# Feed-forward weight sums one column pair ahead, S4 in the buffer of S2, and the evacuation of ad behind the next block's first copy

## The chip, the cores and the metric

The kernel runs as one program on one core of a Trainium2 chip. The core has five engines with a queue each: PE (TensorE), DVE (VectorE), ACT (ScalarE), POOL (GpSimd) and SP (SyncE, which here only issues DMAs). The metric is device time in microseconds (us) of one execution. Before the change it is 3349.23 us, the median of three runs between 3341.76 and 3353.75.

## The reference, cut to what matters

The reference is one inference step of a one-layer encoder: a mixing sub-layer (attention and gated linear attention) and then a gated feed-forward sub-layer. The change lies in the feed-forward alone, on T = 2048 + 32 tokens, D_MODEL = 1024 and D_FF = 2816:

```python
def conv_ffn(h, conv_state, w_up, w_dw, b_dw, w_down):
    t = h.shape[1]
    u = h @ w_up
    uu = jnp.concatenate([conv_state.astype(u.dtype), u], axis=1)
    y = b_dw
    for j in range(CONV_W):
        y = y + w_dw[j] * uu[:, j:j + t]
    a, g = jnp.split(y, 2, axis=-1)
    out = (jax.nn.gelu(a, approximate=True) * g) @ w_down
    return out, uu[:, -(CONV_W - 1):]
```

All is float32. Each float32 operand of a product is split into a high and a low part, and a product is three passes (high times high, high times low, low times high).

## The kernel before, in words

**Units and blocks.** The tokens are cut into six segments, and two segments are worked on at a time (p = 0, 1, 2). Both feed-forward matrices are multiplied by a Strassen-like scheme: the weight matrix is seen as 2x2 quarters A11, A12, A21, A22, the activations as quarters B, and a pair of output columns over a pair of segments takes seven products instead of eight. The seven weight operands are A11, A12, A22 and four sums: S1 = A21 + A22, S2 = S1 - A11, S3 = A11 - A21, S4 = A12 - S2. A *block* is one pair of output columns m of one unit u. Units 0 to 2 are the up-projection for p = 0, 1, 2 with 22 blocks each; units 3 to 11 are the down-projection, for each p in three groups of rows, with 4 blocks each. That is 102 blocks; each has seven products of 12 matmuls (9 where a group has three row tiles).

**The weights of a column.** The generator `weights()` (L1476) serves the operands. The first time a column is met (p = 0: unit 0 and units 3 to 5, 34 columns, called *fresh* below) SP loads the four quarters from HBM (L1490) into four of eight raw buffers (`raws`, 256 KB each), POOL makes S1, S2 and S3 (L1512, three instructions, S3 in the place of A21), and DVE makes S4 in the place of A12 (L1512). Every operand is then split: the high part by ACT (L67), the low part by DVE (L70), into slots named ring, hA and hB. The four sums are stored to HBM (sW, sD; L1515) and loaded again for p = 1 and p = 2, where neither POOL nor the S4 subtraction has work. POOL's three sums of a column stand at the start of the column's own turn in this generator, and they write buffers that S4 (once A12) and A22 of the column before have just left.

**A block** (L1644 to L1699) runs on two accumulators in PSUM, `ad` and `g`. Product A11 goes to ad; ACT copies it to g (L1656); then follows A22, the last product of the block before, into that block's g, with its convolution and gating on ACT and DVE (`up_g`, L1607); then S2 to g, a copy of g to U2 (L1662), S1 to ad, a copy P5 (L1665), S3 to g, an add on DVE (L1668), A12 to ad, S4 to ad, an add on DVE (L1679). After it the block's ad is evacuated: in the up-projection a convolution of width 3 (ACT L1575, then twice DVE L1577) and a gelu on ACT (L1687); in the down-projection a sum into an accumulator (`down_sum`, L1620). Every second block `act_sums` (L1599 to L1602) makes sums of two columns of activations on DVE in place, which must wait until the store of those activations has landed. Seven times in a block `side()` lets the work beside the blocks take one step: stores that were put off (L1590), the rest of the mixing sub-layer at the start, one step of `weights()` (one split), one step of the activation operands, and the work after a unit.

**What sets the order.** PE's order is written out by hand (a manual schedule for that engine alone). For ACT, DVE, POOL and SP a scheduler sets the order from the program. Within an engine instructions run in that order, one after the other.

Of the kernel before, what the change touches and what calls it, by code (L numbers as in the profile page):

```python
# [26 lines left out]
MF = 22  # L27
# [31 lines left out]
def encoder_step(ctx: ExitStack, tc: tile.TileContext, I, O):  # L59
# [520 lines left out]
    with ExitStack() as st:  # L580
# [188 lines left out]
        def step(gen):  # L769
            if gen is not None:  # L770
                next(gen, None)
# [690 lines left out]
    def raw(i, n=4):  # L1462
        return raws_[:, 512 * i:512 * i + 128 * n].rearrange("p (k n) -> p k n", n=128)
# [12 lines left out]
    def weights():  # L1476


        todo = []
        for u, (p, g) in enumerate(UNITS):  # L1480
            for m in range(NM[u]):
                todo += [(u, m, x) for x in (("A21", "A22", "A11", "A12") if p == 0 else WOPS)]
        at = {}

        def fetch():

            while todo and free and len(at) < NRAW - 2:
                u, m, x = todo.pop(0)
                at[u, m, x] = i = free.pop(0)
                nc.sync.dma_start(raw(i, NK[u]), w_rows(u, m, x))  # L1490

        freed = []

        def refill():

            free.extend(freed)
            freed.clear()
            fetch()

        def part(u, m, x, i):  # L1500
# [9 lines left out]
        def total(u, m, eng, op, out, a, b):  # L1510
            n = NK[u]
            getattr(eng, op)(raw(out, n), raw(a, n), raw(b, n))  # L1512

        def keep(u, m, x, i):
            nc.sync.dma_start(w_rows(u, m, x), raw(i, NK[u]))  # L1515

        fetch()
        for u, (p, g) in enumerate(UNITS):
            for m in range(NM[u]):
                if p == 0:  # L1520
                    a11, a12, a21, a22 = [at.pop((u, m, x)) for x in ("A11", "A12", "A21", "A22")]
                    free.extend(freed)
                    freed.clear()
                    s1, s2 = free.pop(0), free.pop(0)
                    total(u, m, nc.gpsimd, "tensor_add", s1, a21, a22)
                    total(u, m, nc.gpsimd, "tensor_sub", s2, s1, a11)
                    total(u, m, nc.gpsimd, "tensor_sub", a21, a11, a21)
                    fetch()
                    for x, i in zip(WOPS, (a11, s2, s1, a21, a12, a12, a22)):
                        if x == "S4":  # L1530
                            total(u, m, nc.vector, "tensor_sub", a12, a12, s2)
                            freed.append(s2)
                        yield from part(u, m, x, i)
                        if x == "S1":
                            keep(u, m, "S2", s2)
                        if x in SUM and x != "S2":
                            keep(u, m, x, i)
                        yield
                        refill()
                        if x not in ("S2", "A12"):  # L1540
                            freed.append(i)
                else:
                    for x in WOPS:
                        i = at.pop((u, m, x))
                        yield from part(u, m, x, i)
                        yield
                        refill()
                        freed.append(i)

    wq = weights()  # L1550

# [55 lines left out]
    def up_g(p, m, g, ya, before):  # L1607

        o = WP[p] - 2
        conv(YG, g, m + MF, o)  # L1610
        nc.vector.tensor_mul(ya[:, :, :o], ya[:, :, :o], YG[:, :, :o])
        defer(1, actD[p, m, :, :, :o], ya[:, :, :o])
        if m % 2:
            made.append((p, m // 2, before, ya))
# [29 lines left out]
    def block(u, m, prev, side):  # L1644
# [24 lines left out]
        last = u == len(UNITS) - 1 and m == NM[u] - 1  # L1669
        if last:  # L1670
            down_sum(p, grp, m + 4, g, False, 1)
        if u == 2:
            conv_outputs(g[:, 1], m + MF)
# [6 lines left out]
        if u == 2:  # L1680
            conv_outputs(ad[:, 1], m)
        if grp is None:
            YA.append(YA.pop(0))
            before, ya = YA[-2:]
            o = w - 2
            conv(ya, ad, m, o)
            nc.scalar.activation(ya[:, :, :o], ya[:, :, :o], AF.Gelu_apprx_tanh)  # L1687
        else:
# [96 lines left out]
    def hstep():  # L1785
        while hq and next(hq[0], 1) == 1:
            hq.pop(0)
# [137 lines left out]
```

## Time and profile before

| | us |
|---|---|
| median of three runs | 3349.23 |
| profiled execution, device time | 3328.72 |
| its span, first to last instruction | 3327.0 |
| mean granted TensorE clock in it | 0.981 |
| PE busy, share of the span | 3134.7, 94% |
| DVE busy | 2264.7, 68% |
| ACT busy | 1673.4, 50% |
| POOL busy | 573.0, 17% |

All times in the rows below are from this one execution. The feed-forward takes from about 1813 us to the end. Unit 0 with its 22 blocks lies between about 1840 and 2209 us, unit 1 between 2209 and 2514, unit 2 between 2514 and 2819, units 3 to 5 begin at 2819. PE's clock is full (1.00) in most of it, and the busy share of PE is high, so what can be had lies in the stretches where PE waits.

### The profile page before, as it was taken

How to read it: one execution, taken by the hardware profiler on the slowest of the kernel's cores; microseconds unless marked ns; L12 is line 12 of the kernel's file. 1: busy time of each engine (PE TensorE's matmuls, PEld its weight loads, DVE VectorE, ACT ScalarE, POOL GpSimd, SP SyncE). 2: the span in 40 equal slices, each digit the busy share in tenths (PEclk: the TensorE clock that was granted, in tenths of full speed). 3: DMA queues.
4: the chain of work that ended last, by engine and by line, in shares of the span. 5: the costliest groups of instructions: out<-in, count | busy, mean ns of one | idle time of the engine just before them, and what ended most of it. 6: DMA issues, size and time to landing. Idle time of an engine off the chain costs nothing. (4 is left out here: it accounts for less than half of the span.)

```text
span 3327.0 us, 58007 instructions
## 1 busy us (share of the span) xinstructions
PE 3134.7 (94%) x19928; PEld 2979.6 (90%) x19928; DVE 2264.7 (68%) x4858; ACT 1673.4 (50%) x3835; POOL 573.0 (17%) x687
## 2 busy tenths in 40 slices
PE   6999999999999999899999798999999999899996
PEld 5899998888999999889988787999999999899996
DVE  6725527664545555754777887887778778788886
ACT  4412224443455545533545644465556656566755
POOL 3102101111111111112444323210000001221011
PEclk8999999999999999999999999999999999999998
DMA  7334434445333333654565786576668666769794
GB/s 216 113 121 142 128 110 120 126 129 138 107 109 113 111 106 114 206 169 155 166 213 172 234 263 223 189 238 193 185 183 242 192 191 194 232 208 294 222 284 125
DMA packets 601370, 580.25 MB, mean 174 GB/s; under 512 B 55761, under 2 KB 529570, under 8 KB 601074
## 3 DMA queue, kind: packets, MB, share of 16 engines
q1 hardware_dynamic: 556386, 528.93, 53.1%
q10 hardware_dynamic: 44432, 47.34, 4.4%
q8 instruction: 157, 2.57, 0.3%
q14 instruction: 139, 1.14, 0.1%
q0 software_dynamic: 256, 0.26, 0.0%
HBM read 388.71 MB, written 187.65 MB: 173 GB/s over the span
## 5 line engine op out<-in xcount | busy, mean ns | idle before, releaser
L76 PE MATMUL pm<-hA,wh 128*128 128x416 f32 x768 | 288.2, 375 | 0.0
L67 ACT ACTIVATE hA<-raws 128x512 fp32r<-128x512 f32 (+1 forms) x320 | 196.5, 617 | 180.7 <-PE ad L1561 96.8
L77 PE MATMUL pm<-hA,wh 128*128 128x416 f32 x768 | 269.4, 351 | 0.0
L78 PE MATMUL pm<-hA,wl 128*128 128x416 f32 x768 | 269.2, 351 | 0.0
L1561 PE MATMUL ad<-hA,hB 128*128 128x350 f32 (+2 forms) x1533 | 264.4, 323 | 0.9 <-ACT work L1665 0.7
L1561 PEld LDWEIGHTS ad<-hA,hB 128*128 128x128 f32 x1533 | 249.4, 189 | 1.8 <-ACT work L1665 1.7
L1512 POOL TENSOR_TENSOR raws<-raws 128x512 f32<-128x512 f32 (+1 forms) x102 | 147.6, 1460 | 587.2 <-DVE g L1571 284.6
L70 DVE TENSOR_TENSOR hA<-raws,hA 128x512 fp32r<-128x512 f32 (+1 forms) x320 | 229.6, 720 | 28.0 <-ACT hA L67 26.8
L67 ACT ACTIVATE hB<-raws 128x512 fp32r<-128x512 f32 (+1 forms) x240 | 147.0, 616 | 131.2 <-PE ad L1561 68.0
L934 POOL TENSOR_SCALAR P<-P,mx 128x640 f32<-128x640 f32 (+5 forms) x136 | 101.3, 745 | 544.0 <-DVE mx L933 269.1
L1561 PE MATMUL g<-hA,hB 128*128 128x350 f32 (+2 forms) x954 | 171.8, 330 | 20.4 <-ACT g L1656 9.7
L1561 PE MATMUL ad<-hA 128*128 128x350 f32 (+2 forms) x1047 | 182.9, 325 | 2.0 <-ACT work L1665 2.0
L70 DVE TENSOR_TENSOR hB<-raws,hB 128x512 fp32r<-128x512 f32 (+1 forms) x240 | 168.6, 705 | 22.9 <-ACT hB L67 20.8
L1561 PEld LDWEIGHTS g<-hA,hB 128*128 128x128 f32 x954 | 157.6, 192 | 26.5 <-ACT g L1656 13.4
L76 PE MATMUL pn<-wh,hA 128*128 128x256 f32 (+1 forms) x624 | 177.8, 285 | 0.0
L1561 PE MATMUL ad<-hA,hA 128*128 128x348 f32 (+2 forms) x1014 | 177.8, 325 | 0.0
L78 PE MATMUL pn<-wh,hA 128*128 128x256 f32 (+1 forms) x624 | 176.7, 283 | 0.0
L77 PE MATMUL pn<-wl,hA 128*128 128x256 f32 (+1 forms) x624 | 176.7, 283 | 0.0
L1561 PEld LDWEIGHTS ad<-hA 128*128 128x128 f32 x1047 | 171.8, 191 | 2.3 <-ACT work L1665 2.3
L1561 PE MATMUL ad<-hA,ring 128*128 128x348 f32 (+2 forms) x978 | 169.5, 324 | 1.3 <-ACT work L1665 1.3
L67 ACT ACTIVATE pth<-pp 128x256 fp32r<-128x256 f32 (+1 forms) x288 | 106.1, 373 | 126.3 <-PE pp L1001 116.3
L1561 PEld LDWEIGHTS ad<-hA,hA 128*128 128x128 f32 x1014 | 166.6, 191 | 0.1
(437 smaller groups left out, 9168.9 us busy)
## 6 DMA issues: line engine op xcount, KB each, us to landing
raws<-in_w_up_dram SPq DMA_DIRECT2D x220, 256.0 KB, 3.7
raws<-sW SPq DMA_DIRECT2D x176, 256.0 KB, 3.0
sW<-raws SPq DMA_DIRECT2D x88, 256.0 KB, 3.2
raws<-in_w_down_dram SPq DMA_DIRECT2D x80, 256.0 KB, 4.6
wr<-in_w_in_dram SPq DMA_DIRECT2D x76, 256.0 KB, 3.4
sgT<-tx ACTq DMA_DIRECT2D x80, 208.0 KB, 2.3
wa<-in_w_ada_dram SPq DMA_DIRECT2D x64, 256.0 KB, 3.1
keys<-ks SPq DMA_DIRECT2D x128, 128.0 KB, 2.9
```

Source lines behind the costliest of these rows:

```text
L67: i = nc.scalar.activation(hi, src, AF.Copy)
L70: nc.vector.tensor_sub(lo, src, f32(hi))
L76: nc.tensor.matmul(out, ah, bh, start=first and i == 0, stop=False)
L77: nc.tensor.matmul(out, ah, bl, start=False, stop=False)
L78: nc.tensor.matmul(out, al, bh, start=False, stop=last and i == n - 1)
L934: nc.gpsimd.tensor_scalar(P[:m, :tot], P[:m, :tot], mx[:m, 6:7], 1.0, op0=OP.mult, op1=OP.mult)
L1512: getattr(eng, op)(raw(out, n), raw(a, n), raw(b, n))
L1561: nc.tensor.matmul(out[:, :w], l_[:, k], r_[:, k, :w], start=first and k == 0 and i == 0, stop=k == n - 1 and i == 2, skip_group_check=True)
```

## The change

It has five parts. (1) `weights()` is written anew: POOL's sums of the next fresh column (`total3`) are issued before the S4 split of the current one, and not at the start of their own column; S1 and S2 take the buffers that S3 and A12 of the current column leave. (2) S4 is written into the buffer of S2 and not of A12, right before the split of S3, and every sum is stored as its own split is issued. (3) Loads may run at most to the next column, but may use all eight buffers. (4) In `block()` the convolution (or `down_sum`) of ad moves into `rest()`, which the next block calls after its first copy; the outputs of the convolution's state move with it. (5) In `side()` the step of the activation operands comes before that of the weights.

```diff
+        def total3(c):
+            free.extend(freed)
+            freed.clear()
+            at[c, "S1"], at[c, "S2"] = s1, s2 = free.pop(0), free.pop(0)
+            at[c, "S3"] = a21 = at.pop((c, "A21"))
+            total(c, nc.gpsimd, "tensor_add", s1, a21, at[c, "A22"])
+            total(c, nc.gpsimd, "tensor_sub", s2, s1, at[c, "A11"])
+            total(c, nc.gpsimd, "tensor_sub", a21, at[c, "A11"], a21)
...
-            while todo and free and len(at) < NRAW - 2:
+            while todo and free and todo[0][0] <= cur + 1:
...
-        for u, (p, g) in enumerate(UNITS):
-            for m in range(NM[u]):
-                if p == 0:
-                    a11, a12, a21, a22 = [at.pop((u, m, x)) for x in ("A11", "A12", "A21", "A22")]
-                    free.extend(freed)
-                    freed.clear()
-                    s1, s2 = free.pop(0), free.pop(0)
-                    total(u, m, nc.gpsimd, "tensor_add", s1, a21, a22)
-                    total(u, m, nc.gpsimd, "tensor_sub", s2, s1, a11)
-                    total(u, m, nc.gpsimd, "tensor_sub", a21, a11, a21)
-                    fetch()
-                    for x, i in zip(WOPS, (a11, s2, s1, a21, a12, a12, a22)):
-                        if x == "S4":
-                            total(u, m, nc.vector, "tensor_sub", a12, a12, s2)
-                            freed.append(s2)
-                        yield from part(u, m, x, i)
-                        if x == "S1":
-                            keep(u, m, "S2", s2)
-                        if x in SUM and x != "S2":
-                            keep(u, m, x, i)
...
+        for cur in range(len(cols)):
+            u, m = cols[cur]
+            for x in WOPS:
+                if x == "A11" and fresh[cur] and (cur, "S1") not in at:
+                    total3(cur)
+                if x == "S3" and fresh[cur]:
+
+                    at[cur, "S4"] = at[cur, "S2"]
+                    total(cur, nc.vector, "tensor_sub", at[cur, "S4"], at[cur, "A12"], at[cur, "S4"])
+                if x == "S4" and cur + 1 < len(cols) and fresh[cur + 1]:
+                    total3(cur + 1)
+                i = at[cur, x]
+                yield from part(cur, x, i)
+                if fresh[cur] and x in SUM:
+                    nc.sync.dma_start(w_rows(u, m, x), raw(i, NK[u]))
+                yield
+                refill()
+                if not (fresh[cur] and x == "S2"):
+                    freed.append(i)
...
     def up_g(p, m, g, ya, before):
 
         o = WP[p] - 2
+        if p == 2:
+            conv_outputs(g[:, 1], m + MF)
         conv(YG, g, m + MF, o)
...
-        if u == 2:
-            conv_outputs(ad[:, 1], m)
-        if grp is None:
-            YA.append(YA.pop(0))
-            before, ya = YA[-2:]
-            o = w - 2
-            conv(ya, ad, m, o)
-            nc.scalar.activation(ya[:, :, :o], ya[:, :, :o], AF.Gelu_apprx_tanh)
-        else:
+        if last:
             down_sum(p, grp, m, ad, m == 0)
         side()
 
         def rest():
+            if grp is None:
+                YA.append(YA.pop(0))
+                before, ya = YA[-2:]
+                o = w - 2
+                if u == 2:
+                    conv_outputs(ad[:, 1], m)
+                conv(ya, ad, m, o)
+                nc.scalar.activation(ya[:, :, :o], ya[:, :, :o], AF.Gelu_apprx_tanh)
+            elif not last:
+                down_sum(p, grp, m, ad, m == 0)
             prod(g[:, 0], u, m, "A22", "T4", False)
...
         issue()
         step()
+        hstep()
         next(wq, None)
-        hstep()
         pend()
```

Every engine executes the same number of instructions as before, and PE's order is the same matmul for matmul. What moves on the other engines is shown at three places in the middle of unit 0. (The line numbers shift: POOL's and DVE's sums are at L1512 before and at L1499 after; the copy of ad to g is L1656 and L1654; the convolution on ACT L1575 and L1571, on DVE L1577 and L1573; gelu L1687 and L1688.)

First POOL, with the semaphores each row waits for, the three sums of one column of unit 0. Before:

```order
L1512 TENSOR_TENSOR raws<-raws 128x512 [waits DMAHW6_49,DMAHW7_49,DMAHW2_49,DVE_49]
L1512 TENSOR_TENSOR raws<-raws 128x512 [waits DMAHW2_49,DVE_49,Pool_49]
L1512 TENSOR_TENSOR raws<-raws 128x512
```

And after, the three of the same column:

```order
L1499 TENSOR_TENSOR raws<-raws 128x512 [waits DMAHW1_49,DMAHW0_49,DMAHW4_49,DVE_49,Pool_49]
L1499 TENSOR_TENSOR raws<-raws 128x512 [waits DMAHW3_49,Pool_49]
L1499 TENSOR_TENSOR raws<-raws 128x512 [waits DVE_49]
```

Before, the first row waits for the low part of the previous column's S4 on DVE and for the landing of that S4's store, since it writes S4's buffer. After, the first row waits for the previous column's S3 (its split and its store), and one sum, now S2 in the third row, for the low part of the previous column's A12 on DVE; both splits stand ahead of that of S4, which is the sixth of the column's seven.

Second DVE, in the middle of unit 0 around column 15: `hB_677`, `hA_104` and `ring` are slots of the split operands, L70 is the low part of a split. Before:

```order
L70 TENSOR_TENSOR hB_677<-raws,hB_677 128x512 [waits PE_49,Activation_49]
L1577 SCALAR_TENSOR_TENSOR work<-ad,cw,work 128x2x348 [waits DVE_49]
L70 TENSOR_TENSOR hA_104<-raws,hA_104 128x512 [waits PE_49,Activation_49]
L1577 SCALAR_TENSOR_TENSOR work<-g,cw,work 128x2x348 [waits Activation_49]
L70 TENSOR_TENSOR hA_104<-raws,hA_104 128x512 [waits PE_49,Activation_49]
L1577 SCALAR_TENSOR_TENSOR work<-g,cw,work 128x2x348 [waits DVE_49]
L70 TENSOR_TENSOR ring<-raws,ring 128x512 [waits DMAHW4_49,PE_49,Activation_49]
L1611 TENSOR_TENSOR work<-work 128x2x348 [waits DVE_49]
L1668 TENSOR_TENSOR g<-g,work 128x350 [waits PE_49,Activation_49]
L1600 TENSOR_TENSOR work<-work 128x348 [waits DVE_49]
L1512 TENSOR_TENSOR raws<-raws 128x512
```

And after:

```order
L70 TENSOR_TENSOR hB_677<-raws,hB_677 128x512 [waits PE_49,Activation_49]
L1573 SCALAR_TENSOR_TENSOR work<-ad,cw,work 128x2x348 [waits DVE_49]
L70 TENSOR_TENSOR hA_104<-raws,hA_104 128x512 [waits PE_49,Activation_49]
L1499 TENSOR_TENSOR raws<-raws 128x512 [waits DMAHW4_49,DMAHW0_49,DVE_49]
L1573 SCALAR_TENSOR_TENSOR work<-g,cw,work 128x2x348 [waits Activation_49]
L70 TENSOR_TENSOR hA_104<-raws,hA_104 128x512 [waits PE_49,Activation_49]
L1573 SCALAR_TENSOR_TENSOR work<-g,cw,work 128x2x348 [waits DVE_49]
L70 TENSOR_TENSOR ring<-raws,ring 128x512 [waits PE_49,Activation_49]
L1609 TENSOR_TENSOR work<-work 128x2x348 [waits DVE_49]
L1666 TENSOR_TENSOR g<-g,work 128x350 [waits PE_49,Activation_49]
L1596 TENSOR_TENSOR work<-work 128x348 [waits DVE_49]
```

The sum S4 (L1512, now L1499) moves seven instructions forward, to right behind the low part of S2, and where it had no wait it now waits for two DMAs: the load of A12 and the store of S2.

Third ACT, around the first copy of the same block. Before:

```order
L1575 ACTIVATE work<-ad,cw 128x2x348
L67 ACTIVATE hB_677<-raws 128x512
L1656 COPY g<-ad 128x350
L67 ACTIVATE hA_104<-raws 128x512
L1687 ACTIVATE work<-work 128x2x348
L1575 ACTIVATE work<-g,cw 128x2x348
L67 ACTIVATE hA_104<-raws 128x512
L1662 COPY work<-g 128x350
```

And after:

```order
L1571 ACTIVATE work<-ad,cw 128x2x348
L67 ACTIVATE hB_677<-raws 128x512
L1654 COPY g<-ad 128x350
L67 ACTIVATE hA_104<-raws 128x512
L1688 ACTIVATE work<-work 128x2x348
L1571 ACTIVATE work<-g,cw 128x2x348
L67 ACTIVATE hA_104<-raws 128x512
L1660 COPY work<-g 128x350
```

Here nothing moved: the convolution of ad stands ahead of the first copy as it did. The same holds in the middle of units 0 and 1; in about half the blocks of unit 2 it now stands behind the copy.

On SP the loads and stores are the same ones, with the four loads of a column next to each other and the stores of one S4 and of the next column's S1 to S3 in a row.

## Rows read from the trace of the kernel before

**Rows 1.** The stretches of the feed-forward: start and end in us, length, busy us of PE, PEld, DVE, ACT and POOL with instruction counts, then the granted TensorE clock as a share of full speed, the DMA share and GB/s.

```profile
1840.00:1920.00 80.00, 61.45 (x332) 58.44 (x332) 72.36 (x114) 52.63 (x96) 31.35 (x29) 0.89 0.73 227
1920.00:2057.00 137.00, 119.52 (x684) 116.42 (x682) 114.15 (x165) 65.74 (x110) 37.27 (x34) 0.94 0.79 249
2057.00:2209.00 152.00, 140.00 (x840) 134.80 (x840) 124.48 (x176) 80.95 (x138) 39.38 (x26) 1.00 0.63 199
2209.00:2514.00 305.00, 297.61 (x1842) 294.29 (x1843) 241.96 (x367) 178.26 (x300) 0.27 (x4) 1.00 0.69 199
...
2819.00:2990.00 171.00, 155.24 (x918) 152.30 (x919) 134.75 (x185) 100.99 (x183) 45.93 (x33) 0.96 0.69 215
```

**Rows 2.** The same view for the copy L1656 alone, which is executed once a block: the count in brackets is the number of blocks.

```profile
1840.00:1920.00 80.00, 1.78 (x4) 0.89 0.73 227
1920.00:2057.00 137.00, 3.58 (x8) 0.94 0.79 249
2057.00:2209.00 152.00, 4.46 (x10) 1.00 0.63 199
2209.00:2514.00 305.00, 9.87 (x22) 1.00 0.69 199
...
2819.00:2990.00 171.00, 5.32 (x13) 0.96 0.69 215
```

**Rows 3.** What PE waited for, by stretch (total us, times, longest us): two rows of 1840 to 1920, two of 1920 to 2057, two of 2057 to 2209, one of 2209 to 2514, and two of 2819 to 2990.

```profile
PE g L1561 <- ACT work L1662: 11.7, 4, 5.6
PE g L1561 <- ACT g L1656: 3.7, 3, 1.7
...
PE g L1561 <- ACT g L1656: 7.8, 4, 3.0
PE g L1561 <- ACT work L1662: 5.0, 2, 2.6
...
PE g L1561 <- ACT g L1656: 8.0, 7, 1.7
PE g L1561 <- ACT work L1662: 3.1, 5, 1.5
...
PE g L1561 <- ACT g L1656: 7.3, 8, 1.4
...
PE g L1561 <- ACT work L1662: 11.0, 5, 3.2
PE g L1561 <- ACT g L1656: 5.5, 4, 3.4
```

**Rows 4.** The timeline from 2098.6 to 2106.5 us, a block in the middle of unit 0: start, length, engine, line, operation, and in brackets the idle time before it with what ended it. L1512 on DVE is the sum S4, on POOL S1 to S3 of the next column.

```profile
2098.74 0.68 DVE L1512 TENSOR_TENSOR raws<-raws 128x512 f32<-128x512 f32 x1
...
2099.45 0.34 SPq L1515 DMA_DIRECT2D sW<-raws  x1
...
2103.55 4.34 POOL L1512 TENSOR_TENSOR raws<-raws 128x512 f32<-128x512 f32 x3 [10.74 <-DVE hA L70]
2104.87 0.63 ACT L67 ACTIVATE hB<-raws 128x512 fp32r<-128x512 f32 x1 [1.56 <-POOL raws L1512]
2105.41 0.44 ACT L1656 COPY g<-ad 128x350 f32<-128x350 f32 x1
...
2105.90 0.91 PE L1561 MATMUL g<-hA,hA 128*128 128x350 f32 x4 [0.92 <-ACT g L1656]
```

**Rows 5.** The timeline around 2088 us, the block before that one.

```profile
2087.53 0.52 DVE L1599 TENSOR_TENSOR work<-work 128x348 f32<-128x348 f32 x1 [1.62 <-DMA actD<-work]
2087.97 0.52 DVE L1679 TENSOR_TENSOR ad<-ad,work 128x350 f32<-128x350 f32 x1
...
2088.53 0.93 ACT L1575 ACTIVATE work<-ad,cw 128x696 f32<-128x696 f32 x1 [2.26 <-DVE ad L1679]
...
2090.48 2.20 PE L1561 MATMUL g<-hA,hA 128*128 128x350 f32 x12 [0.90 <-ACT g L1656]
```

**Rows 6.** The timeline from 2837 us, a block of unit 3 (down-projection).

```profile
2838.69 0.63 ACT L67 ACTIVATE ring<-raws 128x512 fp32r<-128x512 f32 x1 [1.32 <-POOL raws L1512]
...
2841.19 0.46 ACT L1662 COPY work<-g 128x348 f32<-128x348 f32 x1
...
2841.70 1.53 PE L1561 MATMUL g<-hA,hA 128*128 128x348 f32 x4 [2.74 <-ACT work L1662]
```

**Rows 7.** What ACT waited for from 1840 to 2209 us (total us, times, longest us), its rows on POOL's sums and on the add L1679.

```profile
ACT work L1575 <- DVE ad L1679: 20.5, 14, 3.1
ACT hA L67 <- POOL raws L1512: 18.8, 16, 3.5
...
ACT hB L67 <- POOL raws L1512: 14.1, 13, 2.7
```

**Rows 8.** DVE and POOL by groups of instructions (count | busy us, mean ns of one | idle us before them and what ended it): two of DVE from 2057 to 2209 us, one of POOL in the same stretch, and the first group of DVE again from 2209 to 2514 us, where POOL makes no sums.

```profile
L70 DVE TENSOR_TENSOR hA<-raws,hA 128x512 fp32r<-128x512 f32 x31 | 24.2, 783 | 5.0 <-ACT hA L67 5.0
...
L1599 DVE TENSOR_TENSOR work<-work 128x348 f32<-128x348 f32 x4 | 2.1, 522 | 4.8 <-DMA actD<-work 4.8
...
L1512 POOL TENSOR_TENSOR raws<-raws 128x512 f32<-128x512 f32 x26 | 39.4, 1530 | 86.5 <-DVE work L1599 30.3 <-DMA sW<-raws 22.5 <-DMA raws<-in_w_up_dram 12.1
...
L70 DVE TENSOR_TENSOR hA<-raws,hA 128x512 fp32r<-128x512 f32 x68 | 46.4, 683 | 2.7 <-ACT hA L67 2.6
```

**Rows 9.** The page's list of DMA issues: count, KB each, median us from issue to landing.

```profile
sW<-raws SPq DMA_DIRECT2D x88, 256.0 KB, 3.2
```

More of the change, by code (lines that the diff above doesn't have):

```diff
@@ L1476, in weights @@
     def weights():
-        todo = []
-        for u, (p, g) in enumerate(UNITS):
-            for m in range(NM[u]):
-                todo += [(u, m, x) for x in (("A21", "A22", "A11", "A12") if p == 0 else WOPS)]
-        at = {}
-        def fetch():
-            while todo and free and len(at) < NRAW - 2:
[L1488 to L1492, printed above, removed]
+        cols = [(u, m) for u in range(len(UNITS)) for m in range(NM[u])]
+        fresh = [UNITS[u][0] == 0 for u, m in cols]
+        todo = [(c, x) for c in range(len(cols)) for x in (("A21", "A22", "A11", "A12") if fresh[c] else WOPS)]
+        at, freed = {}, []
+        cur = -1
+        def fetch():
+            while todo and free and todo[0][0] <= cur + 1:
+                c, x = todo.pop(0)
+                at[c, x] = i = free.pop(0)
+                nc.sync.dma_start(raw(i, NK[cols[c][0]]), w_rows(*cols[c], x))
         def refill():
@@ L1498, in refill, with total, part @@
             fetch()
-        def part(u, m, x, i):
+        def total(c, eng, op, out, a, b):
+            n = NK[cols[c][0]]
+            getattr(eng, op)(raw(out, n), raw(a, n), raw(b, n))
+        def total3(c):
[6 more added lines that the diff above has]
+            total(c, nc.gpsimd, "tensor_sub", a21, at[c, "A11"], a21)
+        def part(c, x, i):
+            u, m = cols[c]
             while True:
@@ L1508, in part @@
             split(hi[:, :n], lo[:, :n], raw(i, n))
[L1510 to L1515, printed above, removed]
-        fetch()
-        for u, (p, g) in enumerate(UNITS):
-            for m in range(NM[u]):
-                if p == 0:
-                    a11, a12, a21, a22 = [at.pop((u, m, x)) for x in ("A11", "A12", "A21", "A22")]
-                    free.extend(freed)
-                    freed.clear()
-                    s1, s2 = free.pop(0), free.pop(0)
-                    total(u, m, nc.gpsimd, "tensor_add", s1, a21, a22)
-                    total(u, m, nc.gpsimd, "tensor_sub", s2, s1, a11)
-                    total(u, m, nc.gpsimd, "tensor_sub", a21, a11, a21)
-                    fetch()
-                    for x, i in zip(WOPS, (a11, s2, s1, a21, a12, a12, a22)):
-                        if x == "S4":
-                            total(u, m, nc.vector, "tensor_sub", a12, a12, s2)
-                            freed.append(s2)
-                        yield from part(u, m, x, i)
-                        if x == "S1":
-                            keep(u, m, "S2", s2)
-                        if x in SUM and x != "S2":
-                            keep(u, m, x, i)
[L1538 to L1541, printed above, removed]
-                else:
[L1543 to L1548, printed above, removed]
@@ new lines, in weights @@
+        fetch()
+        for cur in range(len(cols)):
[16 more added lines that the diff above has]
+                    freed.append(i)
+                del at[cur, x]
+                if x == "S2" and fresh[cur]:
+                    at[cur, "S2"] = i
+            at.pop((cur, "S2"), None)
@@ L1679, in block @@
         nc.vector.tensor_add(ad[:, 1, :w], ad[:, 1, :w], U2[:, :w])
-        if u == 2:
-            conv_outputs(ad[:, 1], m)
-        if grp is None:
-            YA.append(YA.pop(0))
-            before, ya = YA[-2:]
-            o = w - 2
-            conv(ya, ad, m, o)
-            nc.scalar.activation(ya[:, :, :o], ya[:, :, :o], AF.Gelu_apprx_tanh)
-        else:
+        if last:
             down_sum(p, grp, m, ad, m == 0)
```

1 line of the change is left out of this document (removed).

## The prediction

> **What bounds the kernel now.** I read the stretches first. PE's share of a stretch is lowest where columns are fresh: unit 0 and units 3 to 5 [rows 1]. With the block counts [rows 2] the mean block takes 80/4 = 20.0 us from 1840 to 1920, 137/8 = 17.1 us to 2057, 152/10 = 15.2 us to 2209 (call these A, B, C), and 305/22 = 13.86 us in unit 1, where the same seven products run on weight sums that are only loaded. PE's matmuls take 297.61/22 = 13.5 us of a unit 1 block, so PE bounds that unit, and what bounds A, B, C and units 3 to 5 (13 blocks in 171 us, call this E) is something else. The reader is to compare C with unit 1: 1.34 us more a block at the same full clock.
>
> Next, what PE waited for [rows 3]. It is nearly always one of ACT's two copies, A to g (L1656) or g to U2 (L1662): 15.4 us in A, 12.8 in B, 11.1 in C, 16.5 in E. Unit 1 has 7.3 us for 22 blocks, or 3.3 for ten. A copy is short (0.44 us), so the question is what held ACT's queue. In the timeline of a block in C [rows 4] ACT sat 1.56 us until POOL's sum was there, did that split, then the copy, and PE started 0.92 us late. POOL's first sum began at 2103.55 after 10.74 us of rest. The name in its bracket (DVE L70) had been done for some time; what came last is the store of the previous S4, issued at 2099.45 (its landing takes 3.2 us as a median [rows 9], so it was due near 2102.7), because S1 of the next column writes the buffer that S4 leaves. POOL's own group says the same: 22.5 us of its idle time in C ended with sW<-raws [rows 8]. In unit 3 the same wait costs more, 1.32 us on ACT and another further on, and PE 2.74 [rows 6]. Over A to C, ACT waited 18.8 + 14.1 us for POOL's sums in its two larger rows [rows 7].
>
> Not all waits are POOL's. One block earlier [rows 5] DVE stood behind L1599, which waited 1.62 us for a landing; the add L1679 came late, ACT waited 2.26 us for it with the convolution of ad, the copy stands behind that convolution, and PE lost 0.90. I followed each of C's seven L1656 waits in the same manner: four (some 4.4 us) end with POOL, three (some 3.6) with the add, and there a late POOL sum is second.
>
> **The change part by part.** All terms are made against the profiled execution (3328.72 us, span 3327.0, so 1.7 us lie around it). The median of the runs is 3349.23, 0.6% above; I scale by 1.0062 at the end.
>
> *POOL's sums a column ahead.* No instruction is added. In C the first sum no longer waits for S4's store. It waits for S3's, and S2, which the order puts last of the three, for the low part of A12. Before, the sums began at 2103.55 and S2 as the second of three was done after two thirds of 4.34 us, at 2106.4 [rows 4]. After, A12's low part stands ahead of the sum S4 that began at 2098.74, and behind it S2 needs one sum of 1.5 us: 2100.2 or sooner, 6 us earlier. That clears ACT's waits of 0.6 to 1.6 us and leaves the splits to wait only for their slots. In C: POOL's four waits give 4.4 us; if the block goes all the way to unit 1's length it is 13.4. I take -10, with bounds -3 and -13.4, nearer the upper since 11.1 - 3.3 = 7.8 us lie on the two copies [rows 3] and PE's busy time a block also falls from 14.0 towards 13.5 where it runs unbroken. In B, POOL's waits are about 8.5 of the 12.8 us; the half-clock pieces (0.94) would partly go with them. DVE is busy 114.15 of 137, a floor at -20 (14.6 us a block). I take -9, bounds 0 and -20. In A, DVE is busy 72.36 of 80 and other work runs beside; the first column gains nothing: -2, bounds +5 and -6. In E I followed PE's waits too, and those that end with POOL make 9.4 us (the largest but one in rows 6), with DVE at 134.75 of 171 not in the way: -9, bounds -3 and -14.
>
> *S4 in the buffer of S2.* Same subtraction, 0.68 us [rows 4], on DVE earlier by seven instructions. What is new is its wait for the store of S2 to land. Behind it in DVE's queue stand the two convolution steps of g, three low parts and the add L1668, all of which PE waits for in the end. By the reckoning above S2's sum ends at 2100.2, its store lands 3.2 to 4 us later, by 2104.2, and DVE comes to S4 behind the low part of S2, which needs a slot that PE leaves after the copy at 2105.41, or an estimated us sooner where the copy is no longer late. So there are 1 to 2 us of slack. Bounds: nothing, and 34 columns by 3.2 us = 109, if each store were wholly exposed. I take +3, since the wait is covered in the steady state and only the first columns of a unit, where POOL starts late, should pay a store's landing: one in each of four units would be 13, one is 3.
>
> *Loads.* A column's loads come closer together, but not later than the sums before needed them; POOL had 12.1 us of its idle time in C behind loads [rows 8], which falls on the same chain that has now 6 us more. Nothing, bounds -2 and +4.
>
> *Evacuation of ad.* In units 0 and 1 the scheduler leaves ACT's convolution ahead of the copy, so a wait as in rows 5 stays; unit 1's 7.3 us [rows 3] stay too: -0.5, bounds -2 and +1. In half of unit 2's blocks the copy goes first, which frees PE there but lets the convolution, and with it ad's release, come 0.44 us later: +1, bounds +5 and -1 (unit 2 has no row here; the ends are estimates from unit 1's waits). Steps of `side()` in the other order: nothing, hidden behind whichever split is waiting anyway.
>
> Sum: -10 - 9 - 2 - 9 + 3 - 0.5 + 1 = -26.5, so 3328.7 becomes 3302.2, and times 1.0062 **3322 us** for the median.
>
> **One rule weighed.** In C, where POOL sums, a low part on DVE takes 783 ns, in unit 1 683 [rows 8]: they slow each other a little, by 0.1 us of 0.7. The Trainium skill, page "SBUF — State Buffer", section "Who interferes with whom", says that a DVE instruction with two SBUF inputs and a GpSimd instruction that reads SBUF exclude each other wholly, the second standing until the first has ended. By that rule every sum of 1.5 us beside DVE would hold a low part for up to its length, and the mean of the trace is far below; taken as it stands it gives the third rival.
>
> **The rivals.**
> *First: the wait only moves.* With POOL out of the way DVE is the next: it is busy 12.4 of 15.2 us in C, and L1599 with its landing (4.8 us idle ahead of it in C [rows 8]) still holds the add L1679, and ACT's convolution still stands ahead of the copy. For it: 20.5 us of ACT's waits from 1840 to 2209 are on that add, more than on either group of POOL's [rows 7]. Against it: in unit 1 the same add and the same landing cost PE only 7.3 us in 22 blocks. It gives C -2, B -3, E -5, S4 +1: -9, so 3320 and 3340 us.
> *Second, to the other side: S4's new wait takes DVE's time.* If S2's store lands after DVE has come to S4, DVE stands, and with it all that is queued behind. It decides from the point where S2's sum plus a store (3.2 us) is later than the low part of S2 on DVE; S2's low part itself needs only the sum, so if DVE follows POOL closely the whole 3.2 us are exposed. C's block would be DVE's 12.4 + 3.2 = 15.6 against 15.2: +4; B +3, A +5, E +3 = +15: 3344 and 3364 us. For it: DVE's queue has the sum right behind S2's low part; against it, the slack reckoned above.
> *Third: POOL and DVE exclude each other.* In C a block has 39.4/10 = 3.9 us of sums. If DVE stood still in all of them, its 12.4 us less the 0.9 by which the low parts are longer than in unit 1 would become 15.4, and C gains nothing; nor do A and B. Only E stays: -9 + 1: 3321, and 3341 us. The means of rows 8 speak against it.
> *Fourth: more than waits.* C, B and E all reach unit 1's manner, and B and E the full clock: -13 - 20 - 14 and 2 for the rest: -45, and 3304 us. DVE's share in A and B speaks against it.
>
> **How the numbers follow.** Forecast 0.58, its own range 3308 to 3335. First rival 0.18, second 0.13, third 0.06, fourth 0.05. The bound for a measurable difference is 0.3%, here 10 us: below 3339 is faster, above 3359 slower. The first and third rival lie on the lower bound and go half and half. Faster: 0.58 + 0.05 + 0.09 + 0.03 = 0.75, less 0.03 for the forecast's tail; same: 0.12 + 0.03 + 0.01 of the second rival's near side; slower: 0.12. The range from 3300 to 3354 takes in the forecast, the first and the third rival and the near part of the second.
>
> **What would show it.** Right: ACT's rows on POOL's sums [rows 7] shrink to a third or less; PE's waits for the two copies in C fall to 4 us and in E to 8; block lengths of about 14.2 in C and 16 in B; unit 1 unchanged. On POOL no idle time of length that ends with S4's store. If S4's sum on DVE shows idle time that ends with sW<-raws, the second rival has that much; if ACT's convolution waits for the add as long as before and the PE wait stays, the first. If low parts in C go well above 0.8 us, the third. Wrong altogether: PE's waits in unit 0 as before, or a new wait in units 1 and 2, which have no sums to gain from.

## The result and the profile after

The changed kernel takes 3359.3 us (median of five runs, 3355.51 to 3362.35); the kernel before took 3346.15 in five runs beside it. The ratio is 1.0037, with a 95% interval from 1.0021 to 1.0054: slower, by about 13 us, where 26.5 faster was forecast.

The two profiles stand further apart than that: spans of 3353.7 and 3327.0 us. A second profile of the kernel before (a0 below) has 3341.0, so the first one was at the fast end, and stages are compared with both. One profile of a program says a stage's time only roughly: B stands at 136 and 140 in the two profiles of before, and unit 1 at 316 after and at 308 in run b4 below, whose engines execute the same instructions in the same order up to 3009 us, past the end of E. A stage is measured here from one execution of the copy g<-ad to another (the 1st, 5th, 13th, 23rd, 45th, 67th and 79th); A, B, C and E are those of the prediction, "late" is all after E. What lies ahead of A is not in the table; it ends between 1840 and 1852 us in the profiles of this document.

| us | A | B | C | unit 1 | unit 2 | E | late |
|---|---|---|---|---|---|---|---|
| before [rows 1, 2] | 82 | 136 | 152 | 305 | 305 | 171 | 337 |
| before, second profile (a0) | 83 | 140 | 151 | 307 | 308 | 172 | 337 |
| after | 79 | 127 | 164 | 316 | 311 | 167 | 346 |

A, B and E did gain, 22 us against a0 where 20 were forecast. C lost 12 us instead of gaining 10, units 1 and 2 lost 13 and the last part 9. The row of the copy after gives C's ends (first and last start). The stretches that answer to those of before [rows 1] show where the core idled: in the 152 us from 2057 to 2209, which lie in C in both kernels, PE's busy time fell from 140.00 to 133.94 us, DVE's only by 1.8, and the granted clock from 1.00 to 0.97.

```profile
L1654 ACT COPY g<-ad x11: 443/452/452, 2049.1 to 2212.7; 128x350 f32<-128x350 f32 x10, 128x348 f32<-128x348 f32 x1
```

```profile
1920.00:2057.00 137.00, 123.39 (x729) 119.88 (x729) 123.52 (x178) 71.16 (x120) 44.43 (x36) 0.98 0.84 267
2057.00:2209.00 152.00, 133.94 (x791) 131.12 (x790) 122.67 (x164) 75.95 (x127) 36.12 (x23) 0.97 0.58 178
2209.00:2514.00 305.00, 291.15 (x1776) 286.33 (x1774) 229.19 (x348) 166.47 (x281) 0.00 (x0) 0.99 0.68 192
```

What PE waited for after (total us, times, longest), one row of B, one of C, one of unit 1 and two of E, against [rows 3]: the wait for the copy L1654 (L1656 before) doubled in C and in unit 1, and the one for L1660 (L1662 before) shrank in E and left C. Unit 1's part of this is in some measure this execution's: b4 has 10.1 us there, a0 8.7, before 7.3.

```profile
PE g L1557 <- ACT g L1654: 7.2, 6, 2.7
...
PE g L1557 <- ACT g L1654: 18.1, 8, 3.5
...
PE g L1557 <- ACT g L1654: 15.2, 11, 2.3
...
PE g L1557 <- ACT work L1660: 7.5, 4, 2.8
PE g L1557 <- ACT g L1654: 4.5, 2, 2.9
```

What ACT waited for in unit 0 after, against [rows 7]: POOL's sums went from 18.8 to 6.8 us and from 14.1 to 3.0, as forecast; the add on ad (L1675, L1679 before) went from 20.5 to 45.1.

```profile
ACT work L1571 <- DVE ad L1675: 45.1, 15, 4.9
...
ACT hA L67 <- POOL raws L1499: 6.8, 7, 1.4
...
ACT hB L67 <- POOL raws L1499: 3.0, 4, 1.2
```

The timeline of a block of C after shows what holds the add; it answers to [rows 4, 5].

```profile
2133.91 0.69 DVE L1499 TENSOR_TENSOR raws<-raws 128x512 f32<-128x512 f32 x1
...
2134.62 6.80 SPq L1536 DMA_DIRECT2D sW<-raws  x4
...
2136.18 4.90 POOL L1499 TENSOR_TENSOR raws<-raws 128x512 f32<-128x512 f32 x3 [10.86 <-DVE hA L70]
...
2137.95 1.98 DVE L1609 TENSOR_TENSOR work<-work 128x696 f32<-128x696 f32 x1
...
2141.52 0.52 SPq L1586 DMA_DIRECT2D actD<-work  x1
...
2145.51 0.52 DVE L1595 TENSOR_TENSOR work<-work 128x348 f32<-128x348 f32 x1 [3.28 <-DMA actD<-work]
2145.95 0.52 DVE L1675 TENSOR_TENSOR ad<-ad,work 128x350 f32<-128x350 f32 x1
...
2146.51 0.93 ACT L1571 ACTIVATE work<-ad,cw 128x696 f32<-128x696 f32 x1 [4.26 <-DVE ad L1675]
...
2147.86 0.45 ACT L1654 COPY g<-ad 128x350 f32<-128x350 f32 x1
...
2148.36 0.66 PE L1557 MATMUL g<-hA,ring 128*128 128x350 f32 x1 [2.81 <-ACT g L1654]
```

The reader is to follow it upwards. PE is 2.81 us late by the copy, the copy by the convolution, that by the add, the add by L1595 ahead of it on DVE, and L1595 waits for the landing of the activations' store (actD). That store is late twice. The product that makes the activations (L1609) took 1.98 us and ended at 2139.93; the second of POOL's three sums had begun 0.40 us ahead of it. And SP issued the store only at 2141.52, because ahead of it in SP's queue stood the stores of four sums, the last of them that of S2, whose sum (POOL's third) ended at 2136.18 + 4.90 = 2141.08. Before, the product (L1611) took 876 ns and SP issued the store 0.03 us behind it in each of C's ten blocks (start of the store's row less the end of the product's, in the timeline). The block of [rows 4] is one of them:

```profile
2097.08 0.88 DVE L1611 TENSOR_TENSOR work<-work 128x696 f32<-128x696 f32 x1
...
2097.98 0.53 SPq L1590 DMA_DIRECT2D actD<-work  x1
```

After, the store is issued 1.6 us behind the product in eight of C's ten blocks, and 1.33 us as a mean. These are two of DVE's rows of C before (a third, L1599, is in [rows 8]):

```profile
L1611 DVE TENSOR_TENSOR work<-work 128x696 f32<-128x696 f32 x10 | 8.8, 876 | 0.0
...
L1601 DVE TENSOR_TENSOR work<-work 128x348 f32<-128x348 f32 x5 | 2.6, 519 | 2.5 <-DMA actD<-work 2.4
```

After, the product doubled, the waits for its store went from 4.8 and 2.5 us to 14.1 and 8.8, and the new wait of S4 for S2's store (L1499) is 0.3 us in all. One more row doubled, the in-place sum L1596 (L1600 before, 512 ns). It stands ahead of the wait of L1597, in which DVE idles anyway.

```profile
L1609 DVE TENSOR_TENSOR work<-work 128x696 f32<-128x696 f32 x10 | 17.5, 1754 | 0.0
...
L1499 DVE TENSOR_TENSOR raws<-raws 128x512 f32<-128x512 f32 x9 | 6.2, 692 | 0.3
...
L1596 DVE TENSOR_TENSOR work<-work 128x348 f32<-128x348 f32 x5 | 5.2, 1045 | 0.0
...
L1666 DVE TENSOR_TENSOR g<-g,work 128x350 f32<-128x350 f32 x10 | 5.2, 518 | 0.0
L1597 DVE TENSOR_TENSOR work<-work 128x348 f32<-128x348 f32 x5 | 2.6, 522 | 8.8 <-DMA actD<-work 8.8
...
L1595 DVE TENSOR_TENSOR work<-work 128x348 f32<-128x348 f32 x4 | 2.1, 522 | 14.1 <-DMA actD<-work 14.1
```

### The profile page after: what moved, and what is told of

Its sections match the earlier page's. It is cut to its first block, busy times and chain, and to the rows that moved or that the text cites. A ratio compares the mean times of both kernels' runs of the same rounds, so it can differ in the third digit from the quotient of the medians.

```text
span 3353.7 us, 58179 instructions
## 1 busy us (share of the span) xinstructions
PE 3146.0 (94%) x19928; PEld 2986.2 (89%) x19928; DVE 2275.7 (68%) x4858; ACT 1671.5 (50%) x3835; POOL 581.5 (17%) x687
## 5 line engine op out<-in xcount | busy, mean ns | idle before, releaser
L1499 POOL TENSOR_TENSOR raws<-raws 128x512 f32<-128x512 f32 (+1 forms) x102 | 155.6, 1537 | 583.3 <-DVE hB L70 339.0
L70 DVE TENSOR_TENSOR hA<-raws,hA 128x512 fp32r<-128x512 f32 (+1 forms) x320 | 231.2, 725 | 27.2 <-ACT hA L67 24.7
L70 DVE TENSOR_TENSOR hB<-raws,hB 128x512 fp32r<-128x512 f32 (+1 forms) x240 | 178.1, 746 | 15.7 <-ACT hB L67 12.7
```

The lines of the kernel that those rows point to most:

```text
L70: nc.vector.tensor_sub(lo, src, f32(hi))
```

## The experiments

Each ratio is to the kernel before, run beside it; the stages are those of one profiled execution each. Theory at the outset (S in the expectations): the sums' new place harms C through the product and SP's queue. Rivals: the moved evacuation does it (theory E there, not the stage E), or the difference is between executions (theory N).

| run | ratio to before (95%) | C | unit 1 | unit 2 | E | late |
|---|---|---|---|---|---|---|
| a0 before again | 1.0003 (0.9990 to 1.0017) | 151 | 307 | 308 | 172 | 337 |
| a1 weights() alone | 0.9989 (0.9974 to 1.0004) | 166 | 313 | 310 | 159 | 341 |
| a2 block() alone | 1.0018 (1.0003 to 1.0032) | 151 | 310 | 310 | 179 | 338 |
| a3 side() alone | 1.0008 (0.9995 to 1.0022) | 153 | 307 | 306 | 175 | 337 |
| c1 weights() and block() | 1.0029 (1.0015 to 1.0043) | 164 | 313 | 312 | 162 | 344 |
| c2 weights() and side() | 0.9999 (0.9986 to 1.0012) | 166 | 310 | 309 | 161 | 345 |
| b1 a1, actD's store first | 0.9966 (0.9950 to 0.9982) | 153 | 312 | 311 | 160 | 345 |
| d3 a1, sums later | 0.9971 (0.9960 to 0.9981) | 154 | 311 | 308 | 162 | 343 |
| b2 a1, both | 0.9952 (0.9940 to 0.9965) | 147 | 307 | 307 | 162 | 345 |
| d1 changed kernel, both | 0.9966 (0.9954 to 0.9977) | 147 | 310 | 313 | 167 | 346 |
| b4 changed, down_sum undone | 1.0038 (1.0024 to 1.0052) | 165 | 308 | 309 | 167 | 351 |
| b3 a1, act_sums moved | 0.9886 (0.9870 to 0.9903) | 139 | 297 | 298 | 165 | 345 |
| d2 changed, act_sums moved | 0.9864 (0.9848 to 0.9881) | 141 | 295 | 299 | 163 | 347 |
| c4 before, act_sums moved | 0.9922 (0.9904 to 0.9940) | 151 | 296 | 299 | 175 | 339 |
| c3 b2 with act_sums moved | 0.9833 (0.9809 to 0.9858) | 135 | 297 | 299 | 164 | 343 |

### One part of the change at a time

a0 is the kernel before without an edit. a1 puts the new `weights()` into it, a2 the new `block()` and `up_g`, a3 swaps the two steps in `side()`; c1 and c2 are the changed kernel with one part put back.

> The kernel before, unchanged. In the two profiles unit 1 took 304.9 us before and 316.3 after, though its engines' orders are the same row for row and only the landings of the activation stores differ. Theory N (the first profile of before was a lucky execution): unit 1 here takes 308 to 316 us, the span is 3340 or more, stage C (the last ten blocks of unit 0) stays near 152. Theory D (something in the change slows unit 1): unit 1 here takes 305 again and the span 3327. The ratio to before should be 1.000 within 0.002.

> Only the new weights() (sums a column ahead, S4 in the place of S2, loads); block() and side() as before. Theory S (the sums' new place: POOL's sums run beside the product L1609, and the store of S2 stands ahead of the activation store on SP): stage C takes about 162 us as in the changed kernel, stage B about 127; in all 0 to 15 us slower than before. Theory E (the evacuation does the harm): stage C falls to 142 to 148 and the whole is 10 to 25 us faster than before.

> Only the change in block() (convolution or sum of ad behind the next block's first copy in the program, state outputs with it); weights() and side() as before. Theory S: stage C as before, 152, unit 2 some us longer or the same, in all within 5 us of before. Theory E: stage C at 160 or more, or unit 2 and the last units 10 us longer, in all 10 to 20 us slower.

> Only the order of the two steps in side(): activation operands before weights. It reorders the engines only where activation operands are loaded, at the ends of units 0 to 2 and in the down-projection. Theories S and E both: within 4 us of before. If it is 8 us or more slower, the growth of the changed kernel in units 6 to 11 is this edit's.

> The changed kernel with the order in side() undone (weights before activation operands). The three parts alone add up to +0.15% of before, the whole change is at +0.37%; units 3 to 5 took 159 us with the new weights() alone and 167 with all three. If the order in side() is what takes the gain of units 3 to 5 back, this kernel has 158 to 161 us there and is 5 to 10 us faster than the changed one; if block() does, it stays at 166 to 168.

> The changed kernel with block() undone. The counterpart: if block() takes the gain of units 3 to 5 back, they take 158 to 161 us here; if the order in side() does, 166 to 168. Stage C stays at 162 to 167 in both, since its cause is in weights().

C's loss is wholly in `weights()`: 164 to 166 us in every kernel that has the new one as it is, 151 to 153 in every one with the old. So theory S holds for C, and theory E falls there; in all, a2 is 6 us slower by its ratio, between what the two had said. `weights()` alone comes out level with before: its gain in B and E (24 us against a0) is eaten by C (15) and by small losses in unit 1, the last part and the time ahead of A. `block()` costs 0.2% alone and 0.4% beside the new `weights()` (c1 against a1, changed against c2). `side()` comes out at 0.1%, which its interval does not tell from nothing. Theory N was half right: a0's unit 1 is 307, under what was expected, but its span is 3341. c1 and c2 don't settle where E's gain went in the changed kernel: both have 161 to 162, so the 167 belongs to no single part. Nor was it followed up why a2 has 179 in E.

### The two causes in weights()

b1 adds an order edge on SP (issue order alone, no wait) so that S2's store goes behind the activation store that is due; b2 does so for the stores of S1 to S3 and also lets S1 and S2 change buffers, by which POOL's first sum waits for the low part of A12; d3 has the buffers changed without the edge; d1 is the complete changed kernel with both.

```diff
-            at[c, "S1"], at[c, "S2"] = s1, s2 = free.pop(0), free.pop(0)
+            at[c, "S2"], at[c, "S1"] = s2, s1 = free.pop(0), free.pop(0)
...
-                    nc.sync.dma_start(w_rows(u, m, x), raw(i, NK[u]))
+                    st = nc.sync.dma_start(w_rows(u, m, x), raw(i, NK[u]))
+                    if x == "S2":
+                        ref = kept[0]
+                    if x != "S4" and ref:
+                        tc.add_manual_dep(st.ins, ref.ins.name, mybir.DependencyInfo(
+                            mybir.DependencyClass.NoSync, mybir.DependencyReason.DATA), reason="behind")
```

(`kept[0]` is the last store to actD that `issue()` made; in b1 the edge is on S2's store alone.)

> The new weights() alone, with one order edge more: on SP the store of S2 is issued behind the store of the activations (actD) that waits at that time, and not ahead of it. Theory Q (SP's queue: actD's store stands behind S2's store, which waits for POOL's last sum): stage C falls by 1 to 1.6 us a block, from 166 to 150 to 156, DVE's waits for actD in it from 22 to 8 to 12 us. Theory P (the port: POOL's sums double the product L1609 that makes actD, 1.75 instead of 0.88 us): C falls by less than 5, the waits stay above 17, L1609 stays at 1.6 to 1.75 us.

> The new weights() alone with S1 and S2 in each other's buffers and no order edge. In stage C the edge alone gave 153, edge and buffers 147, neither 166. If L1609's doubling and the place in SP's queue add up, C is at 157 to 161 here with the product at 0.88 us; if the buffers alone also bring actD's store forward on SP (the order shows two stores ahead of it where there were four), C is at 147 to 152, and the two causes can't be told apart by this run.

> As the run with the order edge (for all three sums' stores), and S1 and S2 change buffers, so that POOL's first sum waits for the low part of A12 instead of that of S3, some 2 us later, beside L1609's start or behind it. Theory P: L1609 falls to 0.9 to 1.1 us and C falls by another 8 us or more against the run with the edge alone. Theory Q: L1609 may fall, but C changes by less than 4.

> The changed kernel, complete, with the two cures (order edge for the sums' stores; S1 and S2 in each other's buffers). C falls from 163.6 to 146 to 149 and the whole from 1.0037 to 0.998 to 1.000 of before. If the two costs are not what made the changed kernel slower, it stays above 1.002.

The product and the two waits for its store in C, from DVE's groups. The new `weights()` alone (a1):

```profile
L1607 DVE TENSOR_TENSOR work<-work 128x696 f32<-128x696 f32 x10 | 15.3, 1531 | 0.0
...
L1597 DVE TENSOR_TENSOR work<-work 128x348 f32<-128x348 f32 x5 | 2.6, 522 | 7.8 <-DMA actD<-work 7.8
...
L1595 DVE TENSOR_TENSOR work<-work 128x348 f32<-128x348 f32 x4 | 2.1, 522 | 14.2 <-DMA actD<-work 14.2
```

With the edge alone (b1) the product stays long and the waits fall from 22.0 (a1) to 10.3 us; SP issues the store 0.25 us behind the product as a mean:

```profile
L1614 DVE TENSOR_TENSOR work<-work 128x696 f32<-128x696 f32 x10 | 16.4, 1644 | 0.0
...
L1604 DVE TENSOR_TENSOR work<-work 128x348 f32<-128x348 f32 x5 | 2.6, 523 | 5.3 <-DMA actD<-work 5.3
L1602 DVE TENSOR_TENSOR work<-work 128x348 f32<-128x348 f32 x4 | 2.1, 522 | 5.0 <-DMA actD<-work 5.0
```

With the buffers alone (d3) the product is short again, but the store is issued 1.13 us behind it, and 13.9 us of wait are left:

```profile
L1607 DVE TENSOR_TENSOR work<-work 128x696 f32<-128x696 f32 x10 | 8.8, 875 | 0.0
...
L1597 DVE TENSOR_TENSOR work<-work 128x348 f32<-128x348 f32 x5 | 3.2, 645 | 4.1 <-DMA actD<-work 4.1
L1595 DVE TENSOR_TENSOR work<-work 128x348 f32<-128x348 f32 x4 | 2.1, 521 | 9.8 <-DMA actD<-work 9.8
```

With both (b2) 4.3 us are left, and the in-place sum on the same path (L1604, L1595 in a1) now meets POOL's sums itself, 1341 ns against 522:

```profile
L1616 DVE TENSOR_TENSOR work<-work 128x696 f32<-128x696 f32 x10 | 8.8, 876 | 0.0
L1604 DVE TENSOR_TENSOR work<-work 128x348 f32<-128x348 f32 x4 | 5.4, 1341 | 1.3 <-DMA actD<-work 1.3
...
L1606 DVE TENSOR_TENSOR work<-work 128x348 f32<-128x348 f32 x5 | 3.4, 677 | 3.0 <-DMA actD<-work 3.0
```

So C is 166 with neither, 153 and 154 with one, 147 with both: taking away the place in SP's queue gives some 13 us, taking away the product's doubling 12, and both 19. Neither theory alone is the whole; the step from b1 to b2 (6 us) lies between what theory P (8 or more) and theory Q (less than 4) had said. The complete changed kernel with both (d1) is at 0.9966, some 24 us under the changed one by the two ratios, and lower than expected; 17 of them are C's. Its timeline shows the same block as above: the product starts 0.16 us ahead of the first sum and keeps its length, the store follows at once, and PE waits 0.25 us.

```profile
2137.52 0.87 DVE L1618 TENSOR_TENSOR work<-work 128x696 f32<-128x696 f32 x1
2137.68 5.28 POOL L1501 TENSOR_TENSOR raws<-raws 128x512 f32<-128x512 f32 x3 [10.12 <-DMA sW<-raws]
...
2138.42 0.53 SPq L1593 DMA_DIRECT2D actD<-work  x1
...
2145.68 2.19 PE L1564 MATMUL g<-hA,ring 128*128 128x350 f32 x12 [0.25 <-ACT g L1663]
```

### The wait itself off the path

b4 puts `down_sum` of ad back to the block's end. b3, c4, d2 and c3 move `act_sums` behind the evacuation of ad, with the first of its subtractions kept behind what was traced on DVE. In b3 this holds for the down-projection too, and there the last pair of activation sums of p = 2 reads buffers that have been used again, so b3 executes as many instructions but leaves the right sums of that pair out; the others keep the old place where `grp` is not None.

```diff
-        act_sums()
+        if grp is not None:
+            act_sums()
...
         def rest():
+            if grp is None:
+                act_sums()
             prod(g[:, 0], u, m, "A22", "T4", False)
```

> The changed kernel with one part undone: down_sum of ad stands again at the block's end; the up-projection's evacuation stays behind the next copy. The new weights() alone took 159 us in units 3 to 5, the change in block() alone 179, both together 167. Theory E2 (down_sum behind the next block's copy costs there): units 3 to 5 at 157 to 161 and 5 to 10 us faster than the changed kernel, C and unit 1 as in it. If units 3 to 5 stay at 166, the loss is from the side() order or from variation.

> The new weights() alone, and act_sums moved behind the evacuation of ad (into the next block's beginning), so that the add on ad no longer stands behind a wait for actD's landing. If that wait is what carries the delay to PE (theories P and Q both end there), PE's waits for the first copy in C fall from 18 to under 6 us, C to 145 to 150, and unit 1 and unit 2 by 4 to 8 us each: the whole 15 to 35 us faster than before. If the wait is only where DVE happens to stand (rival: PE is held by the splits and DVE's work), C stays above 158.

> The kernel before with act_sums alone moved behind the add on ad. Units 1 and 2 fall to 297 each (-10 each against before). In C, if POOL's late sums are still a limit, 145 to 149 and not 138; units 3 to 5 stay at 171. In all 20 to 28 us under before, and 12 to 20 us above the kernel with all cures; if it equals that one, the new weights() is worth nothing once the wait is off the path.

> The changed kernel, complete, with act_sums moved behind the add on ad (at its old place in the first block of unit 3). Theory W (block() costs by way of the same wait): units 1 and 2 at 297 to 299, C at 138 to 140, the whole 3298 to 3306, level with the new weights() so treated (3303). If block() costs by another way (the copy first, ad later free), unit 2 stays 3 to 6 us above 298 and the whole is 3308 to 3316.

> The new weights() with actD's store ahead of the sums' stores, the sums behind A12's low part, and act_sums behind the add on ad (at its old place in the first block of unit 3). From the runs so far: C 138 (it was 146.9 with the two orders and 138.8 with act_sums moved), units 1 and 2 at 297 each, units 3 to 5 at 160 to 165: 3295 to 3308 us, some 40 us under before. If act_sums' move makes the two other cures needless, it is no faster than the run with act_sums moved (3303).

b4 is a miss: E stays at 167 and the ratio at that of the changed kernel. It could not be otherwise in E: up to 3009 us the engines' orders are those of the changed kernel, so the scheduler gives E one order with either place of `down_sum`, and E's loss is not its doing. With `act_sums` moved, unit 1 takes 295 to 297 us in all four kernels, against 305 to 316 in the others: what unit 1 loses over 296 is that wait. The changed kernel so treated (d2, 3298.9) is level with the new `weights()` so treated (b3, 3303): with the wait off the path `block()` costs nothing, as theory W had it. PE's only wait in d2's unit 1:

```profile
PE g L1557 <- ACT g L1654: 0.7, 1, 0.7
```

C divides the parts. Before with `act_sums` moved (c4) stays at 151: there POOL's late sums are the limit, as the prediction read them. With the sums a column ahead it is 139 to 141 (b3, d2), the 10 us that were forecast, and with the two cures as well 135 (in c3's profile, the fastest of its five executions at 3279.7). c3 takes 3294.45 us, 24 under c4 and 1.7% under before (0.9809 to 0.9858). This version beats both kernels.

## Why the prediction was wrong

**Reading the bound: right.** PE waits for ACT's copies, and these in B, C and E in good part for POOL's sums. ACT's waits for the sums fell as forecast. In the changed kernel B gained 9 to 13 us (9 forecast) and A 3 to 4 (2); E gained 3 to 13 over the kernels with the new `weights()` (9).

**"POOL's sums a column ahead", the term for C: the step that failed.** I priced what the sums stop holding up, and not what stands beside and behind them at the new time. C's -10 became +12. The first price was about right: with the loop named below out of the way, C goes from 151 (c4) to 139 and 141 (b3, d2). On the trace of before the loop through product, store, landing, `act_sums` and add was visible [rows 5], and I had given it the smaller part of C's waits (3.6 us, POOL 4.4). In truth it had no slack, since its waits were there already (4.8 us ahead of L1599 [rows 8] and 2.5 ahead of L1601). Two costs were put on that loop: the product's 0.88 us and 1.3 us in SP's queue as means, 2.2 a block, 22 in ten blocks. Most of it reached PE; C came out 17 to 19 us above the versions with both removed (d1, b2). The meeting could have been read from the trace of before: I put the three sums of some 1.5 us so that the last ends by 2100.2, and the product began at 2097.08.

**"Loads ... Nothing" and the queues.** For SP I priced only the loads. That four stores of sums now stand in a row on SP was known, but I did not ask what is queued behind the last of them, which waits for POOL's third sum.

**"One rule weighed": dismissed by a mean.** I set the page's rule aside because low parts of a split take 783 ns in C and 683 in unit 1 [rows 8]. That mean is over instructions beside the sums and others that are not; the rule speaks of single ones. In C before, 21 low parts begin while a sum is under way. They take 0.91 to 1.68 us, and each ends some 0.55 us behind the end of that sum; the others of the same shape take 0.68 to 0.69. One of the 21:

```profile
2088.13 4.67 POOL L1512 TENSOR_TENSOR raws<-raws 128x512 f32<-128x512 f32 x3 [10.72 <-DVE work L1599]
...
2088.41 1.55 DVE L70 TENSOR_TENSOR hB<-raws,hB 128x512 fp32r<-128x512 f32 x1
```

The product shows the same after: 0.88 us alone, 1.97 to 1.98 in the eight blocks of C where it starts 0.4 to 0.6 us after a sum has begun, and 0.87 to 0.88 where it starts 0.16 us ahead of one (d1). The Trainium skill, page "SBUF — State Buffer", section "Who interferes with whom", says that such a DVE instruction and a GpSimd instruction that reads SBUF contend for a shared port, and that the order of issue decides which of them blocks. The trace agrees with both. The sign I had named for the third rival, low parts well above 0.8 us, could not tell: their mean stayed at 0.78 while the product doubled. The third rival had the mechanism, but with the price on DVE's sum of work, and so let C break even; it lies on one instruction of the critical loop.

**"S4 in the buffer of S2": right.** +3 was taken. DVE's idle time ahead of the sum S4 is 2.9 us over all 34 columns (1.4 of it in B, 0.3 in C, 1.2 in E), where it was 4.1 before; how much of it reaches PE was not measured. The second rival falls.

**First rival: nearest.** The wait did move to the add behind L1599 (now L1595), but it grew past the old one, where the rival let it stay.

**Block count.** E has 12 blocks and not 13: the 13th copy in [rows 2] is the one that ends the stretch. No term hangs on it.

**"Evacuation of ad": mis-sized.** -0.5 and +1 were taken for units 1 and 2; `block()` costs 6 to 13 us by the ratios. That it costs by way of the same wait is shown by d2, where it costs nothing. My reading is that a convolution that starts behind the copy makes the activations later; where in each unit this enters was not tried apart, and so it is not shown.

**Not foreseen and open.** Unit 1 runs 307 to 316 us with the new `weights()` and 305 to 310 with the old, though in its middle the engines' order is the same. What differs there is how long DVE waits for the store's landing. Some of this is between executions, since the same order gave 316 (after) and 308 (b4); whether the rest is the change's was not settled. The part after E takes 341 to 351 us in the runs with the new `weights()` and 337 to 339 in those with the old; that was not followed up.

## What to carry to other kernels

Moving work to an idle engine "for free" has two prices beside its own time: what it holds up beside it at the new time, and what stands behind its DMAs in an issuing queue. Look for the loop that has no slack (here product, store, landing, in-place sum, add), and ask of each instruction on it whether the moved work now touches it; read single instructions there, not the mean of their group. The better cure was to take the wait off the path: it gave 26 us to the old kernel and some 58 to the changed one.

## What the runs showed of the hardware

- A DVE product of two SBUF operands (128x696) takes 0.88 us alone and 1.97 to 1.98 when one of POOL's sums (1.3 to 1.9 us each) is under way as it starts; it ends some 0.74 us behind the end of that sum. The add L1666, one of whose operands lies in PSUM, kept its 0.52 us in the eight blocks of C after in which it began beside a sum.
- A DMA that waits on SP holds those behind it: the store of actD was issued 1.6 us behind its product in eight of C's ten blocks after, and 0.03 us behind it where no waiting store stood ahead of it.
- The landing of the activations' store (348 KB) kept DVE waiting 38 and 41 us in unit 1 in two executions of the kernel before, and 47 (after) and 42 (b4) in two with one and the same order of instructions.
